# Six pairs of merge gates by seven block products, and 33 convolution taps by ScalarE and adding transfers, in a decoder layer on one core

## The chip, the core and the metric

The kernel runs on one core of a Trainium2 chip. Its engines are TensorE (PE in the profile, with its weight loads as PEld), VectorE (DVE), ScalarE (ACT), GpSimd (POOL) and SyncE (SP), which mostly issues transfers. The metric is the device time of one execution in microseconds (us). Three runs of the kernel before gave 833.68 to 834.18 us, with a median of 833.92.

## What is computed

One layer of a hybrid decoder trunk for 512 tokens (T) of width 1024 (D), all in float32. Cut to what matters here:

```python
u = rmsnorm(h, norm1_g)
a_glu, q, k, v, r, g_low, gate_a, gate_b = split(u @ w_in)

c = a_glu[..., :1024] * sigmoid(a_glu[..., 1024:])
c = causal_depthwise_conv(c, conv_dw_w, conv_dw_b)      # 31 taps along the tokens
c = silu(layernorm(c, conv_ln_g, conv_ln_b))
y_conv = c @ w_conv_out

o = gated_linear_attention(q, k, v, g_low)              # 4 heads, chunks of 64
y_gla = (head_rmsnorm(o) * silu(r)) @ w_gla_out

merged = sigmoid(gate_a) * y_conv + sigmoid(gate_b) * y_gla
h = h + merged @ w_o

u2 = rmsnorm(h, norm2_g)
z = causal_depthwise_conv(u2 @ w_ffn_up)                # 3 taps, 5632 columns
h = h + (silu(z[..., :2816]) * z[..., 2816:]) @ w_ffn_down
out = rmsnorm(h, final_g)
```

## The kernel before

**Precision.** Every product of float32 matrices is made of three matmuls (`mm3`, L405 to L407): each operand is split into a high part, the value rounded by a cast on ACT, and a low part, the difference taken by DVE; high x low, low x high and high x high are summed in PSUM.

**A plain tile** (`col_tile`, L409) makes 128 columns of a projection for all 512 tokens, channels in the partitions: eight blocks k of 128 input channels, three matmuls of 128x512 each, so 24 matmuls into one PSUM bank. `acts1` are the split activations u, `acts2` those of the FFN. The weight of a tile is one block of 128x1024 (512 KB), loaded by SP into a `raw` tile (four buffers); `split_weight` (L323) casts it into `whi` on ACT and subtracts into `wlo` on DVE (four buffers each).

**The order of the work** is written out in a list `order` of (weight, tile). `weight()` (L372) checks the list off, splits the weights up to two tiles ahead (LOOK) and then calls `fill(RATE)`. `refill` keeps four loads ahead, or two where `few` is true (in the seven-product part of the FFN, whose pairs need several raw tiles at once). The framework puts each engine's instructions in an order of its own within these bounds.

**The filling work.** `chains` is a list of lists of small operations for DVE that PE does not wait for at once. Each `fill(RATE)` puts some into the program, in turns from the first two chains: 31 taps of the depthwise convolution for each of 8 channel blocks (`conv_tap`, L703: the first by ACT into the tile `conv[k]`, the other 30 by DVE, at L711, one multiply-add each), and when all taps are done the chain of the convolution's norm (`norm_chain`, L796): sums over channels, mean on PE, centering and squares (L764, L770), variance on PE, 1/sigma by POOL (L455) and spread over the partitions by PE (L748), then for each block a multiply on DVE (L782), silu on ACT (L784), a cast on ACT and a subtract on DVE (L792, L793), which give `ca[k]`, the operand of w_conv.

**Stages on PE**, one after the other: the input's norm and u; half of v; 16 tiles of w_glu (the convolution's input); w_low and the decay gates (four activations at L841, exponentials at L845, logarithms at L847); the other half of v; four heads of gated attention with their w_qk and w_r tiles; then the merge; w_o; the FFN.

**The merge** (plain tiles only): four w_gb tiles in the last head; then eight w_gla tiles in turns with the last four w_gb; eight w_ga; eight w_conv. The sigmoids (L1021, L1030) are on ACT, the products with y on DVE. Each w_conv tile needs all eight blocks `ca[k]`, block by block in the order of its matmuls. `while chains: fill(1)` ahead of w_conv puts what is left of the chains into the program.

**Seven products.** A product of two 2x2 block matrices can be had from seven block products in place of eight. w_o and w_down are computed so (`seven`, L1075). In the FFN's up projection `up_pair` (L1308) does it for a pair of tiles: the weight blocks are combined by POOL (`up_sums`, L308, additions at L310) into x1, x3, x2 and x4 (x4 is half a block), the activations into s1, n2, s4 and n3 (`sum_acts`, L1248), and PE makes 7 x 4 x 3 = 84 matmuls of 128x256. Between the steps PE has halves of plain tiles, so that the copies (L1315) and combinations (L1318) of one step lie beside them. The combinations are put into the plan by `up_plan` (L147), with the kinds of unit "opens", "closes" and one without a name.

**Adding transfers.** A transfer issued by POOL can add to what stands at its destination (`accum_op`). The kernel before uses it to combine weight blocks of w_o and w_down (L300, L301), from DRAM into SBUF.

Of the kernel before, what the change touches and what calls it, by code (L numbers as in the profile page):

```python
# [17 lines left out]
P = 128  # L18
# [16 lines left out]
AHEAD = 4  # L35
LOOK = 2
# [30 lines left out]
def trunk_layer(ctx: ExitStack, tc: tile.TileContext, a: dict, out: bass.AP):  # L67
# [79 lines left out]
    def up_plan(gi):  # L147
# [8 lines left out]
        def unit(q, f, kind):  # L156
# [35 lines left out]
    def up_order(plan):  # L192
        out = []
        for what, i, *rest in plan:
            if what == "part":
                out.append(("w_up7", (i, rest[0])))
# [10 lines left out]
    order += [("w_gb", m) for m in range(AHEAD)]  # L207
    for m in range(KT):
        order += [("w_gla", m)] + [("w_gb", m + AHEAD)] * (m + AHEAD < KT)
    order += [("w_ga", m) for m in range(KT)]  # L210
    order += [("w_conv", m) for pair in O_PAIRS for m in pair]
    order += [("w_o", (O_PAIRS, step, d)) for step, d in STEPS]
    for gi, pairs in enumerate(GROUPS):
        if gi == 0:
            order += [("w_up", j) for i in pairs[0] for j in (i, FT + i)]
            first7 = len(order) + 6
        order += up_order(up_plan(gi))
        order += [("w_down", (pairs, step, d)) for step, d in STEPS]
# [6 lines left out]
    def load():  # L225
        if len(raws) < len(order):
# [4 lines left out]
            if name == "w_up7":  # L231
                q, part = j
                if part == "x1":
                    pair_raws[q] = [raw_tile() for _ in range(2)]
                    for raw, m in zip(pair_raws[q], (q, FT + q)):
                        nc.sync.dma_start(raw, a["w_up"][m])
# [6 lines left out]
    def refill():  # L243

        while len(raws) < len(order):
            few = len(raws) >= first7 and order[len(raws)][0] != "w_down"
            if len(raws) >= len(ready) + (2 if few else 4):
# [55 lines left out]
    def up_operand(q, part):  # L303

        raws = pair_raws[q]
        return {"x1": lambda: raws[0], "x3": lambda: raws[2], "x2": lambda: raws[1], "x4": lambda: raws[2][:, :T]}[part]()

    def up_sums(q, part):  # L308
# [3 lines left out]
        if part == "x1":  # L312
            one, two = pair_raws[q]
            three = raw_tile()
            pair_raws[q].append(three)
# [3 lines left out]
        if part == "x3":  # L319
            one, _, three = pair_raws[q]  # L320
            add(three[:, left], three[:, right], one[:, right])

    def split_weight(halves=False, between=None):  # L323

        if len(ready) < len(order):
# [4 lines left out]
            if name in SEVEN or name == "w_up7":  # L330
                raw = operand(raw, *spec) if name in SEVEN else up_operand(*spec)
# [5 lines left out]
                sum_on(name, *spec) if name in SEVEN else up_sums(*spec)  # L337
# [34 lines left out]
    def weight(name, j, ahead=LOOK):  # L372
# [4 lines left out]
        fill(RATE)  # L377
# [6 lines left out]

    def fill(n):
        room[0] += n
        while chains and room[0] > 0:
            room[1] += 1
            chain = chains[room[1] % min(2, len(chains))]
# [4 lines left out]
            if not chain:  # L394
                chains.remove(chain)
                if not chains and after:
# [304 lines left out]
    conv = [None] * KT  # L701

# [10 lines left out]
    for k in range(KT):  # L713
# [5 lines left out]
        nc.vector.tensor_tensor(c, pa, sg, ALU.mult)  # L719
        chains.append(  # L720
            [(1 if tap < CW - 1 else 0, lambda k=k, tap=tap, c=c: conv_tap(k, tap, c)) for tap in reversed(range(CW))]
        )

# [269 lines left out]

    heads = [Head(h) for h in range(HEADS)]
    for h in range(HEADS + 1):
# [7 lines left out]
        if old:  # L1003
            old.scores(heads[h - 2].gated if h > 1 else None)
        new.keys() if new else gate_b(1)
# [10 lines left out]

    part = [None] * KT
    ma = [None] * KT
    for m in range(KT):
        part[m] = heap()  # L1020
        nc.scalar.activation(part[m], gbs.pop(m), AF.Sigmoid)  # L1021
        py = col_tile(weight("w_gla", m), oa)
        if m + AHEAD < KT:
            gate_b(m + AHEAD)
        nc.vector.tensor_tensor(part[m], py, part[m], ALU.mult)
    gas = {}
    for m in range(KT):
        pg = col_tile(weight("w_ga", m), acts1)
        gas[m] = heap()
        nc.scalar.activation(gas[m], pg, AF.Sigmoid)  # L1030
    while chains:
        fill(1)
    H = T // 2

    def merged(m):
        sg = gas.pop(m)
        py = col_tile(weight("w_conv", m), ca)
        nc.vector.tensor_tensor(sg, py, sg, ALU.mult)
        nc.vector.tensor_tensor(sg, sg, part[m], ALU.add)
        return sg  # L1040
# [203 lines left out]


    seven_acts = {}

    def sum_acts():  # L1248


        def f32(x):
            return x.bitcast(F32)

        def part(t, k):
            return [u2[k][j][:, :, t * H : (t + 1) * H] for j in range(2)]

        a11, a12, a21, a22 = part(0, 0), part(0, 1), part(1, 0), part(1, 1)

        def tile(pool, tag, bufs, k=4):
            return pool.tile([P, k, H], F32R, tag=tag, name=nm(tag + "s"), bufs=bufs)  # L1260

        def chain(engine, out, start, *terms):

            for op, x in terms:
                engine.tensor_tensor(out, start if start.dtype == F32 else f32(start), f32(x), op)
                start = out
            return out

        def split_sum(src, his, lo):
            n = 4 // len(his)  # L1270
            for j, hi in enumerate(his):
                ks = slice(j * n, (j + 1) * n)
                nc.scalar.copy(hi, src[:, ks])
                nc.vector.tensor_tensor(lo[:, ks], src[:, ks], f32(hi), ALU.subtract)
            return [hi[:, k, :] for hi in his for k in range(n)], [lo[:, k, :] for k in range(4)]

        add, sub = ALU.add, ALU.subtract
        lo = {"n3": tile(fp, "us", 3), "s1": tile(fp, "us", 3), "n2": tile(fp, "us", 3), "s4": tile(tp, "x", 3)}
        hi = {"n3": [tile(tp, "btmp", 2, 2) for _ in range(2)], "s1": [tile(tp, "x", 3)]}
        hi |= {"n2": [tile(tp, "x", 3)], "s4": [tile(tp, "gain", 1)]}  # L1280

        def room(_):
            return keep_tile("w_down").rearrange("p (k t) -> p k t", k=4)

        src = {step: room(step) for step in ("s1", "n2")}
        chain(nc.vector, src["s1"], a21[0], (sub, a22[0]), (add, a21[1]), (sub, a22[1]))
        chain(nc.vector, src["n2"], src["s1"], (sub, a11[0]), (sub, a11[1]))
        yield
        for step in ("n2", "s1"):
            seven_acts[step] = split_sum(src[step], hi[step], lo[step])  # L1290
        yield
        src |= {step: room(step) for step in ("s4", "n3")}
        chain(nc.vector, src["s4"], src["n2"], (add, a12[0]), (add, a12[1]))
        chain(nc.vector, src["n3"], a11[0], (sub, a21[0]), (add, a11[1]), (sub, a21[1]))
        yield
        for step in ("n3", "s4"):
            seven_acts[step] = split_sum(src[step], hi[step], lo[step])
        for step, x in (("a11", a11), ("a12", a12), ("a22", a22)):
            seven_acts[step] = [[y[:, k, :] for k in range(4)] for y in x]
        yield  # L1300

    def up_step(acc, step, w, half, opens):
        ah, al = seven_acts[step]
        for k in range(4):
            s = slice(half * T + k * P, half * T + (k + 1) * P)
# [239 lines left out]
```

## Time and profile before

| | |
|---|---|
| median of three runs | 833.92 us (833.68 to 834.18) |
| the profiled execution | 833.95 us |
| its span | 832.2 us |
| granted clock of PE | 0.998 |
| w_gla's first matmul | 286.7 us |
| w_conv's first matmul | 398.0 us |
| last block of the convolution's norm ready | 399.6 us |
| w_o's first matmul | 441.5 us |

The profile is of one execution. Its page shows the busy time of each engine, the chain of work that ended last (followed back from the last instruction: at each step to what released it), the costliest groups of instructions by line, and the transfers. The trace behind it answers further questions: the waits of an engine by what ended them, the rows of a stretch of time (start, duration, engine, line, operation, output and inputs), and busy time by stage. L405 is line 405 of the kernel. A row's duration can overlap with the next row's, above all on PE; the spacing of starts is then what one costs.

### The profile page before, as it was taken

The page shows a single profiled execution, that of the slowest core. Times are in us where ns is not written, and L with a number is a line of the kernel's source. Part 1 is how long each engine was busy: PE and PEld are TensorE (multiplying, and loading weights), DVE is VectorE, ACT ScalarE, POOL GpSimd, SP SyncE. Part 2 cuts the span into 40 slices and gives each one's busy share as a digit, 9 for nine tenths or more (in the row PEclk, how much of TensorE's full clock was granted, in tenths as well). Part 3 has the DMA queues.
Part 4 walks back from the last instruction along what each step waited for, and adds up shares of the span by engine and source line. Part 5 has one row for each costly group of instructions (what it writes and reads, how often), then busy time and mean ns, then how long its engine had stood idle before and what let it go on. Part 6 is the DMA issues. An engine that isn't in the chain of part 4 may idle for free.

```text
span 832.2 us, 10782 instructions
## 1 busy us (share of the span) xinstructions
PE 822.1 (99%) x4109; PEld 699.8 (84%) x4109; DVE 697.7 (84%) x982; ACT 417.7 (50%) x597; POOL 98.1 (12%) x97
## 2 busy tenths in 40 slices
PE   9999999999999999999999999999999999999996
PEld 7888888888888888888888898898889888889885
DVE  5689879999998799745678889989985999789896
ACT  6723337547533422349544546556435564466654
POOL 2000000000001100000001100230133301513011
PEclk9999999999999999999999999999999999999999
DMA  8223232332212323323337623046632456224662
GB/s 313 101 99 103 84 104 80 98 102 76 93 65 96 117 86 101 102 76 101 102 85 221 190 86 102 26 158 168 143 123 93 142 137 162 104 93 165 174 126 101
DMA packets 28307, 97.82 MB, mean 118 GB/s; under 512 B 3209, under 2 KB 3345, under 8 KB 28257
## 3 DMA queue, kind: packets, MB, share of 16 engines
q1 hardware_dynamic: 24800, 85.35, 30.2%
q0 software_dynamic: 3456, 11.80, 8.4%
q8 instruction: 32, 0.52, 0.3%
q14 instruction: 19, 0.15, 0.1%
HBM read 95.03 MB, written 2.10 MB: 117 GB/s over the span
## 4 chain that ended last, share of the span: by engine, by line
PE 86%; DVE 5%; DMA 4%; issue 2%; ACT 1%; POOL 0%; SPq 0%; POOLq 0%; ACTq 0%; DVEq 0%
PE mm L405 24%; PE mm L406 24%; PE mm L407 24%; PE mm L617 3%; PE ax L405 2%; PE ax L407 2%; PE ax L406 2%; DMA kept<-in_w_o_dram 2%; DVE tmp L1199 1%; DVE wlo L336 1%; DMA raw<-in_w_down_dram 1%; DMA hres<-in_x_dram 1%; PE ax L958 1%; DVE hres L1119 1%; PE ax L960 1%
## 5 line engine op out<-in xcount | busy, mean ns | idle before, releaser
L405 PE MATMUL mm<-uh,wlo 128*128 128x512 f32 (+1 forms) x696 | 261.6, 376 | 0.0
L406 PE MATMUL mm<-ul,whi 128*128 128x512 f32 (+1 forms) x696 | 259.3, 373 | 0.0
L407 PE MATMUL mm<-uh,whi 128*128 128x512 f32 (+1 forms) x696 | 259.0, 372 | 0.0
L362 ACT CAST whi<-raw 128x1024 fp32r<-128x1024 f32 x98 | 102.5, 1048 | 126.3 <-PE mm L407 82.2
L711 DVE SCALAR_TENSOR_TENSOR c<-h,pp,c 128x511 f32<-128x511 f32 (+14 forms) x240 | 162.5, 729 | 0.7
L363 DVE TENSOR_TENSOR wlo<-raw,whi 128x1024 fp32r<-128x1024 f32 x98 | 123.3, 1261 | 35.6 <-ACT whi L362 35.4
L407 PEld LDWEIGHTS mm<-uh,whi 128*128 128x128 f32 x696 | 131.0, 188 | 23.3
L405 PEld LDWEIGHTS mm<-uh,wlo 128*128 128x128 f32 x696 | 131.2, 189 | 22.3
L406 PEld LDWEIGHTS mm<-ul,whi 128*128 128x128 f32 x696 | 131.2, 188 | 22.0
L336 DVE TENSOR_TENSOR wlo<-raw,whi 128x1024 fp32r<-128x1024 f32 (+1 forms) x56 | 65.0, 1167 | 16.5 <-ACT whi L335 12.6
L335 ACT CAST whi<-raw 128x1024 fp32r<-128x1024 f32 (+1 forms) x56 | 53.8, 964 | 28.2 <-PE mm L407 21.3
L310 POOL TENSOR_TENSOR raw<-raw,raw 128x512 f32<-128x512 f32 x24 | 38.3, 1597 | 144.6 <-DVE wlo L336 65.4
L335 ACT CAST whi<-kept 128x1024 fp32r<-128x1024 f32 (+1 forms) x32 | 31.8, 996 | 33.6 <-DVE kept L294 14.4
L1199 DVE SCALAR_TENSOR_TENSOR tmp<-mm,pp,tmp 128x511 f32<-128x511 f32 (+1 forms) x56 | 41.3, 740 | 4.6 <-ACT tmp L1197 4.5
L336 DVE TENSOR_TENSOR wlo<-kept,whi 128x1024 fp32r<-128x1024 f32 (+1 forms) x32 | 36.9, 1153 | 5.9 <-ACT whi L335 5.7
L455 POOL TENSOR_TENSOR rstd<-var,mhalf 128x2 f32<-128x2 f32 (+1 forms) x12 | 12.0, 1006 | 220.5 <-DVE var L965 196.3
L1119 DVE TENSOR_TENSOR hres<-hres,mm 128x512 f32<-128x512 f32 (+1 forms) x49 | 32.3, 669 | 1.7 <-PE mm L407 0.8
L1197 ACT ACTIVATE tmp<-mm,pp 128x512 f32<-128x512 f32 x28 | 21.7, 775 | 20.5 <-PE mm L407 20.4
L1199 DVE SCALAR_TENSOR_TENSOR tmp<-tmp,pp,tmp 128x511 f32<-128x511 f32 (+1 forms) x32 | 27.1, 904 | 0.1
L407 PE MATMUL mm<-whi,sh 128*128 128x512 f32 x66 | 25.7, 389 | 0.0
L406 PE MATMUL mm<-wlo,sh 128*128 128x512 f32 x66 | 25.7, 389 | 0.0
L405 PE MATMUL mm<-whi,sl 128*128 128x512 f32 x66 | 25.5, 389 | 0.0
(305 smaller groups left out, 1496.2 us busy)
## 6 DMA issues: line engine op xcount, KB each, us to landing
raw<-in_w_up_dram SPq DMA_DIRECT2D x44, 512.0 KB, 3.5
raw<-in_w_glu_dram SPq DMA_DIRECT2D x16, 512.0 KB, 3.6
raw<-in_w_down_dram SPq DMA_DIRECT2D x15, 512.0 KB, 4.2
kept<-in_w_down_dram POOLq DMA_DIRECT2D x10, 512.0 KB, 6.1
raw<-in_w_v_dram SPq DMA_DIRECT2D x8, 512.0 KB, 4.2
raw<-in_w_qk_dram SPq DMA_DIRECT2D x8, 512.0 KB, 3.3
raw<-in_w_r_dram SPq DMA_DIRECT2D x8, 512.0 KB, 3.3
raw<-in_w_gb_dram SPq DMA_DIRECT2D x8, 512.0 KB, 3.3
```

The lines of the kernel that those rows point to most:

```text
L310: add = lambda out, x, y: nc.gpsimd.tensor_tensor(out, x, y, ALU.add)
L335: nc.scalar.copy(hi, raw)
L336: nc.vector.tensor_tensor(lo, raw, hi.bitcast(F32), ALU.subtract)
L362: nc.scalar.copy(hi, raw)
L363: pace[0] = nc.vector.tensor_tensor(lo, raw, hi.bitcast(F32), ALU.subtract)
L405: nc.tensor.matmul(acc, ll, rh, start=first, stop=False, **kw)
L406: nc.tensor.matmul(acc, lh, rl, start=False, stop=False, **kw)
L407: nc.tensor.matmul(acc, lh, rh, start=False, stop=last, **kw)
L617: nc.tensor.matmul(acc, act, ready[k // 2][wi][:, j], start=first, stop=last)
L711: nc.vector.scalar_tensor_tensor(y[:, s:], c[:, : T - s], w, y[:, s:], ALU.mult, ALU.add)
L1119: nc.vector.tensor_tensor(hres[t, n][:, c], hres[t, n][:, c], acc[:, c], op)
L1199: nc.vector.scalar_tensor_tensor(z[:, s:], acc[:, : T - s], w[j], z[:, s:], ALU.mult, ALU.add)
```

## The change

It has two parts, with their consequences for the order.

1. **Gates by seven products.** Twelve of the sixteen gate tiles (w_gb 4 to 7, w_ga 0 to 7) are made as six pairs by seven products of 128x256 blocks, each pair in turns with two plain tiles cut into halves: the first three pairs with w_gla 2 to 7, the other three with w_conv (0 and 2, 1 and 3, 4 and 6). So w_conv begins in the fourth pair, and the last two w_conv tiles follow the pairs. The sums of activations s1, n2, s4 and n3 of u are made in pieces put into the program by `fill` ahead of the chains (`urgent`), in the last head and after. `up_pair`, `up_step`, `up_sums`, `up_operand` and `sum_acts` become `two_tiles`, `step_of_two`, `two_sums`, `two_operand` and `token_sums_7`, which the FFN uses as well.

2. **33 taps off DVE.** At each `fill`, while more than two convolution chains are there, up to two of the chains behind the first two give one tap to `tap_by_dma`: ACT multiplies the input by the tap's weight into one of two `products` buffers, and POOL issues a transfer that adds it to `conv[k]` (256 KB, from SBUF to SBUF). A chain that was served so rests for DVE until the next turn.

Besides: the number of chain operations for each tile changes (1.5 for a step of a pair, 6 for w_glu, 4 in the stretches with pairs, 5 elsewhere); loads are two ahead in all stretches with pairs; the FFN's unit "closes" cuts its first tile at 5 and 7 in place of 3 and 6; and the FFN's sums are placed after each "first" and "second".

```diff
+MERGE = [("w_gb", 4 + 2 * j, 5 + 2 * j, ("w_gla", 2 + 2 * j), ("w_gla", 3 + 2 * j)) for j in range(2)]
+MERGE += [("w_ga", 0, 1, ("w_gla", 6), ("w_gla", 7))]
+MERGE += [("w_ga", 2 * j + 2, 2 * j + 3, *(("w_conv", m) for m in O_PAIRS[j])) for j in range(3)]
+MERGE_REST = [("w_conv", m) for m in O_PAIRS[3]]
...
-                a1, a2, a3 = (("tile", a, ks) for ks in halves(3, 6))
+                a1, a2, a3 = (("tile", a, ks) for ks in halves(5, 7))
...
-    for m in range(KT):
-        order += [("w_gla", m)] + [("w_gb", m + AHEAD)] * (m + AHEAD < KT)
-    order += [("w_ga", m) for m in range(KT)]
-    order += [("w_conv", m) for pair in O_PAIRS for m in pair]
+    order += [("w_gb", m) for m in range(AHEAD)] + [("w_gla", m) for m in range(2)]
+    tight = set()
+    first = len(order)
+    for name, p, q, a_, b_ in MERGE:
+        x1, x3, x2, x4 = (("two", (name, p, q, part)) for part in ("x1", "x3", "x2", "x4"))
+        order += [x1, a_, x3, x2, b_, x4]
+    tight |= set(range(first, len(order)))
+    order += MERGE_REST
...
-        fill(RATE)
+        fill({"two": 1.5, "w_glu": RATE + 1}.get(name, RATE - (used[0] - 1 in tight)))
...
     def fill(n):
         room[0] += n
+        while urgent and room[0] > 0:
+            share, work = urgent.pop(0)
+            room[0] -= share
+            with tc.issue_after(pace[0].ins):
+                work()
+        if chain_of:
+            taps_by_dma(chains[2:])
         while chains and room[0] > 0:
             room[1] += 1
-            chain = chains[room[1] % min(2, len(chains))]
+            two = [chain for chain in chains[:2] if id(chain) not in resting] or chains[:1]
+            chain = two[room[1] % len(two)]
...
+    products = tp.tile([P, 2, T], F32, tag="gain", name=nm("products"), bufs=1)
+    turn, last = [0], [[]]
+
+    def taps_by_dma(waiting):
+
+        waiting = sorted((c for c in waiting if id(c) not in last[0]), key=len)[-2:]
+        resting[:] = [*last[0], *map(id, waiting)]
+        last[0] = [id(c) for c in waiting]
+        for chain in waiting:
+            tap_by_dma(chain)
+
+    def tap_by_dma(chain):
+
+        k = chain_of[id(chain)]
+        while chain[0][0] == 0:
+            chain.pop(0)[1]()
+        tap = len(chain) - 1
+        chain.pop(0)
+        n = T - (CW - 1 - tap)
+        turn[0] += 1
+        y = products[:, turn[0] % 2, :n]
+        w = pp[:, PP_CW + k * CW + tap : PP_CW + k * CW + tap + 1]
+        with tc.issue_after(pace[0].ins):
+            nc.scalar.activation(y, conv_in[k][:, :n], AF.Copy, scale=w)
+        nc.gpsimd.dma_start(conv[k][:, T - n :], y, accum_op=ALU.add)
...
+        s1 = chain("s1", a21[0], (sub, a22[0]), (add, a21[1]), (sub, a22[1]))
+        n2 = chain("n2", "s1", (sub, a11[0]), (sub, a11[1]))
+        s4 = chain("s4", "n2", (add, a12[0]), (add, a12[1]))
+        n3 = chain("n3", a11[0], (sub, a21[0]), (add, a11[1]), (sub, a21[1]))
+        return acts7, [s1 + n2, split_sum("s1"), s4, split_sum("n2"), split_sum("s4"), n3, split_sum("n3")]
...
+    def pair_7(name, p, q, a_, b_):
+        unit = two_tiles(name, p, q, lambda: merge_acts, mm_bank)
+        low, high = range(KT // 2), range(KT // 2, KT)
+        if a_[0] == "w_conv":
+            while chains:
+                fill(1)
+        next(unit)
+        acc = tile_of(*a_, low)
+        next(unit)
+        tile_of(*a_, high, acc)
+        next(unit)
+        acc = tile_of(*b_, low)
+        for m, c in zip((p, q), next(unit)):
+            (part if name == "w_gb" else gas)[m] = sigmoid(m, c)
+        tile_of(*b_, high, acc)
+
+    for spec in MERGE[:3]:
+        pair_7(*spec)
```

Each `next(unit)` makes one step of the pair: x1 with two of the seven products, x3 with two, x2 with two, x4 with one.

More of the change, by code (lines that the diff above doesn't have):

```diff
@@ L1014, in trunk_layer @@
     late_scope, late = scoped("late", 1, "right")
+    for work in merge_sums[2:]:
+        urgent += work
     part = [None] * KT
[L1018 to L1024, printed above, removed]
-        nc.vector.tensor_tensor(part[m], py, part[m], ALU.mult)
[L1026 to L1030, printed above, removed]
@@ L1243, in second_of_pair @@
         return acts
[L1246 to L1300, printed above, removed]
```

232 lines of the change are left out of this document (166 added, 66 removed).

## The prediction

> **What bounds the kernel now.** I read the busy totals first, then the chain that ended last, then the waits of TensorE (PE), then single stages in the timeline.
>
> ```profile
> PE 822.1 (99%) x4109; PEld 699.8 (84%) x4109; DVE 697.7 (84%) x982; ACT 417.7 (50%) x597; POOL 98.1 (12%) x97
> ...
> PE 86%; DVE 5%; DMA 4%; issue 2%; ACT 1%; POOL 0%; SPq 0%; POOLq 0%; ACTq 0%; DVEq 0%
> ```
>
> PE is busy in 99% of the span and makes 86% of the chain. What it waited for, in the view of PE's waits (total, times, longest):
>
> ```profile
> PE mm L523 <- DVE ones L496: 1.1, 1, 1.1
> PE ax L531 <- DMA x<-in_x_dram: 0.8, 1, 0.8
> PE mm L405 <- ACT tmp L1315: 0.7, 2, 0.4
> PE ax L484 <- DVE ul L489: 0.3, 1, 0.3
> ```
>
> That is 2.9 us in 832.2, nearly all before 10 us and after 475 us. In the merge PE waits for nothing, so matmul time taken out there counts one for one, unless another engine becomes late. The profiled execution took 833.95 us, its span 832.2 (1.75 us lie outside); the median of the runs is 833.92, so the sum below may stand against either.
>
> **Part 1, the seven products.** Their price is in the trace, since the FFN of the kernel before already works in this way. PE starts, us:
>
> ```profile
> 538.64 0.39 PE L406 MATMUL mm<-ul,whi 128*128 128x512 f32 x1
> 538.87 0.39 PE L407 MATMUL mm<-uh,whi 128*128 128x512 f32 x1
> 539.10 0.28 PE L405 MATMUL mm<-uh,wlo 128*128 128x256 f32 x1
> 539.21 0.28 PE L406 MATMUL mm<-ul,whi 128*128 128x256 f32 x1
> ...
> 541.97 0.40 PE L405 MATMUL mm<-uh,wlo 128*128 128x512 f32 x1
> ```
>
> The second column overlaps (pipelined), so I take spacings. 512 columns: 538.87 - 538.64 = 0.23 (0.2267 over a long run). 256 columns: 24 in 541.97 - 539.10 = 2.87, or 0.1197 each. A plain tile is 24 x 0.2267 = 5.44. A pair by seven is 7 x 12 = 84 narrow matmuls, 84 x 0.1197 = 10.05, in place of 2 x 5.44 = 10.88. The saving is 0.83 by product; from one x1 to the next x1 the FFN shows 560.14 - 539.10 = 21.04 for a pair with two plain tiles in halves, against 4 x 5.44 = 21.76: 0.72. I take 0.72, which holds the switches. Six pairs: **-4.3 us**. The matmul count of everything else is the same.
>
> What the pairs add on other engines. VectorE (DVE) forms the sums of the activations (14 operations of 128x1024 at a spacing of 1.14 = 16 us), 1.7 us more of weight splitting per pair (3.5 in place of 2 at 1.14), and 1.0 of combining (3 at 0.34). ScalarE (ACT) gets 1.5 us of casts and 1.3 of copies per pair, and 4 us for the sums. POOL gets four additions per pair (1.3 to 2.3 each, L310), on an engine that is 12% busy. Each pair with its two plain tiles lasts 21 us on PE. In the first pair DVE's own work (splits 6.3, sums, combines, chain) comes to about 25 us in those 21, but in the trace the wlo splits there run 17 to 20 us ahead of PE's use (250 to 290 us), so 5 to 8 us of lead remain: **0**.
>
> DVE loses some of its speed beside POOL:
>
> ```profile
> 543.73 1.30 POOL L310 TENSOR_TENSOR raw<-raw,raw 128x512 f32<-128x512 f32 x1 [10.03 <-DVE wlo L336]
> ...
> 544.15 1.43 DVE L1210 TENSOR_TENSOR w<-tmp,tmp 128x512 f32<-128x512 f32 x1
> ```
>
> The same L1210 takes 0.75 us elsewhere, so one collision costs about 0.7, and four in each pair would cost 24 x 0.7 = 17. The view of busy time by stage shows what is free there (columns: stage, its length, then busy time of PE, PEld, DVE, ACT, POOL):
>
> ```profile
> 286.00:398.00 112.00, 112.00 (x508) 93.06 (x507) 77.95 (x106) 55.59 (x70) 1.01 (x1) 1.00 0.28 90
> 398.00:441.00 43.00, 43.00 (x191) 35.63 (x190) 31.67 (x49) 17.66 (x24) 1.94 (x2) 1.00 0.41 107
> ```
>
> DVE has 34 + 11 = 45 us free there, and gets 32 more (16 + 10 + 6) less the taps of part 2. I keep 0; if that cover fails, the norm is late (part 3).
>
> **Part 2, 33 convolution taps off DVE.** They are what makes room for those sums:
>
> ```profile
> L711 DVE SCALAR_TENSOR_TENSOR c<-h,pp,c 128x511 f32<-128x511 f32 (+14 forms) x240 | 162.5, 729 | 0.7
> ```
>
> Spacing in a run of them is 0.65 us, so 33 give back 21.5 us. Summed over the program DVE goes from 663.9 to 675.7 us of such durations: still 84% or so of the span, in other places. In return ACT multiplies 33 times (0.6 to 0.7 each by its 128x512 activations) and POOL issues 33 adding transfers of 256 KB. No transfer from SBUF to SBUF is in the trace. The nearest are POOL's adding transfers of weights:
>
> ```profile
> raw<-in_w_down_dram POOLq DMA_DIRECT2D x1, 256.0 KB, 3.6
> kept<-in_w_down_dram POOLq DMA_DIRECT2D x1, 256.0 KB, 7.8
> ```
>
> 3.6 us from issue to landing alone, 7.8 behind others. I take 3.6, since mostly one or two fly; both ends stay. There are two buffers of products, so a multiply waits until the transfer two before it has landed, and a transfer waits for the one before it on its chain. Queued behind a waiting multiply on ACT are the casts whi, and PE waits for those. The tightest place is the gates: three taps stand between the four L841 activations, and two landings in a row are ahead of the last. In the trace the four start at 131.94; by 3.6 the last starts near 137.8, then two table loads (1.28 each), eight activations (2.20 per four) and the cast whi, now near 147.6 for a tile PE reaches at 153.4. With the cast, the subtract and DVE's queue ahead of it, some 2 us are left: **0** at 3.6, a wait from about 4.6 on. Later taps (six of the last chain, 155 to 180 us) have over 7 us.
>
> The Trainium skill, page "SBUF — State Buffer", section "SBUF: two separate sides", speaks against such transfers: descriptors of a POOL-queued DMA are made by GpSimd and starve while a DVE operation in a two-port mode holds the port they share. In this trace such issues take 0.84 to 0.9 us with DVE at work, a few 1.06 to 1.25, so starvation is not seen; by the page the slower rival's sum below would come out, by the row the sum is unchanged.
>
> **Part 3, the order of the merge.** In the trace the convolution's norm is finished only just in time. First ACT, then DVE, from the spread of 1/sigma (L748) on:
>
> ```profile
> 371.72 1.28 ACT L784 ACT_TABLE_LOAD   x1
> 373.01 1.52 ACT L784 ACTIVATE btmp<-c,pp 128x512 f32<-128x512 f32 x2
> 374.44 1.12 ACT L792 CAST ch<-btmp 128x512 fp32r<-128x512 f32 x2
> ```
>
> ```profile
> 370.95 1.29 DVE L782 TENSOR_TENSOR c<-ax,c 128x512 f32<-128x512 f32 x2 [4.49 <-PE ax L748]
> ...
> 398.87 0.69 DVE L793 TENSOR_TENSOR c<-btmp,ch 128x512 fp32r<-128x512 f32 x1
> ```
>
> The first w_conv tile starts at 398.0 and the last normed block is ready at 399.56, 29 us after the spread at 370.0. After the change the w_conv tiles stand among the pairs: the first comes at 286.7 (first w_gla) + 43.5 (eight w_gla tiles at 5.44) + 30.2 (three pairs at 10.05) + 2.9 (the next x1) = 363.3, some 35 us earlier, and the norm must come earlier too. The spread (call its end T) now stands in the third pair, before a half tile (2.75), x4 (1.43), a half (2.75) and the next x1 (2.87): the first convolution block is wanted at T + 9.8. The eighth is wanted after 27 more wide and 24 narrow matmuls: 27 x 0.2267 + 24 x 0.1197 = 9.0, so T + 18.8 to 19.2. ACT needs from T on: a cast whi (0.96), a table load (1.28), two silu (1.43), two casts (1.05), a copy (0.3); then the next whi, whose buffer comes free when PE is done with x4 and a half tile, T + 7.4; then 0.96, a load 1.28, two sigmoids 1.0, a load 1.28, two silu and the casts: the third block at T + 13.9, wanted at T + 12.2; the rest (two silu, two casts, whi, copy, twice more) ends at T + 21.6. **PE waits 1.7 us at the third block and 3.0 in all by the eighth.** The ends: 0, if the scheduled spread runs ahead of this (PE reaches it late, ACT having been idle), and 3.1. I take 2.4, midway between 1.7, which follows from the first load of tables, and 3.0, which needs every later step in its place.
>
> SP's queue holds 175 instructions as before. The kept w_o loads move behind the w_conv loads in it, since the sums hold their buffers until the last pair; the w_o loads land in 3.3 to 5.8 us there, and are due later than that by my count: 0. In the FFN the halves of one kind of unit are cut at 5 and 7 and not 3 and 6: same matmuls, 0.
>
> **Sum**: 833.95 - 4.3 + 2.4 = **832.0 us**.
>
> **Rivals.**
> - All is hidden: no wait at w_conv, 833.95 - 4.3 = **829.6**. For it: waits in the merge are nil now and ACT is half idle. Against it: the chain above is a row of dependent steps.
> - DVE is late in the merge as well: the sums, the collisions with POOL and the norm (two 0.6 us passes over eight blocks) share DVE, so T slips against PE. One collision each in the norm's sums, centering and last multiplies makes 3 x 0.7 = 2.1 more: **834**, no change.
> - Slower: ACT is held by the landings. It decides above 4.6 us from issue. At 7.0 (two in flight) the last gate activation is 2 x 3.4 = 6.8 later, less the 2 us left: 4.8, and PE stands still that long at 153 us; with the sum, 832.0 + 4.8 = **836.8**. For it: 7.8 in the row above. Against it: that transfer was queued behind two larger ones.
>
> **How the numbers follow.** 0.2% (1.7 us) is about what a measurement can tell from no change: faster is below 832.25, slower above 835.6. The forecast has 0.42, of which about two thirds lie below 832.25; all hidden 0.18; DVE late 0.15; landings 0.25. Faster 0.46, same 0.29, slower 0.25. The range runs from 829.4 to 836.8, which leaves out half of the landings' case and a little on the other side.
>
> **What would show it.** Right: x1 to x1 of 21.0 us with two plain tiles in the merge; a wait of PE for ch or c in the first w_conv tile of 1.7 to 3; no wait of PE at 150 to 195 us. Wrong: PE waiting for whi or wlo near 153 us, transfers c<-products landing in over 4.6 us; L363 late in the first pair; or more than 3 us before the first w_conv tile.

## The result, and the profile after

The changed kernel takes 849.22 us (median of four runs, 847.97 to 849.66) against 834.05 for the kernel before: the ratio is 1.0177, with an interval of 1.0159 to 1.0195. The forecast was 832.0, with a range up to 836.8; it is slower by 15 us where a small gain was expected.

The profiled execution of the changed kernel took 849.16 us, its span 847.4, so 15.2 us more than the span before. Busy times, the chain by engine, and two groups of the page (line, engine, operation, tiles and count; busy, mean ns of one; idle time before it and what ended most of it):

```profile
PE 823.8 (97%) x4325; PEld 705.9 (83%) x4325; DVE 720.1 (85%) x1001; ACT 452.1 (53%) x669; POOL 165.9 (20%) x154
...
PE 69%; DVE 12%; DMA 6%; issue 6%; ACT 5%; POOL 1%; POOLq 0%; SPq 0%; ACTq 0%; DVEq 0%
...
L747 POOL DMA_DIRECT2D c<-products x33 | 28.9, 899 | 143.2 <-ACT products L746 112.1
...
L746 ACT ACTIVATE products<-h,pp 128x511 f32<-128x511 f32 (+9 forms) x33 | 23.3, 717 | 43.1 <-DMA c<-products 43.1
```

PE's share of the chain fell from 86% to 69%. The last line names the new thing: ScalarE (ACT) stood still for 43.1 us ahead of 18 of its 33 multiplies, each time until a transfer `c<-products` had landed. PE's waits in the changed kernel, the four largest (total, times, longest):

```profile
PE mm L425 <- DVE wlo L373: 5.7, 4, 2.2
PE ax L886 <- DVE h L877: 2.8, 1, 2.8
PE ax L988 <- ACT kt L968: 2.1, 1, 2.1
PE ax L1023 <- ACT o L1017: 1.6, 1, 1.6
```

None of these is in the list of before. In the stage of the gates and the first head they end at 132.5, 152.2, 160.0, 173.6 and 195.0 us. To place all losses I add up, from the trace's PE rows, what the spacing of successive matmuls exceeds its usual value (0.227 us for 512 columns, 0.120 for 256). This is what PE lost, by stage, in us (differences of under 1 us mean little); the medians are beside it:

| kernel | median | 128-200 us (gates, v, first head) | 200-310 (other heads) | 360-410 (norm and first w_conv tiles) |
|---|---|---|---|---|
| before | 834.05 | 0.5 | 1.5 | 0.2 |
| changed | 849.22 | 15.1 | 5.1 | 1.7 |
| e1, taps on DVE | 854.91 | 0.5 | 3.9 | 18.4 |
| e4, no transfers | 836.44 | 0.5 | 6.1 | 1.6 |
| e10, three pairs, nine taps | 833.77 | 0.5 | 2.3 | 0.2 |
| e14, no transfers, first pair later | 831.63 | 0.5 | 1.6 | 0.8 |
| e15, transfers apart | 850.03 | 14.9 | 6.3 | 1.7 |
| e16, the same, memset on DVE | 838.43 | 0.5 | 8.8 | 1.7 |

Over the whole span the changed kernel lost 20.0 us more of this than before (25.2 against 5.2), and its span grew by 15.2, so the seven products gave back 4.8, near the 4.3 of the forecast. Their rate is in the trace, PE rows of the changed kernel from one x1 to the next (start, duration):

```profile
314.94 0.28 PE L425 MATMUL mm<-uh,wlo 128*128 128x256 f32 x1
...
335.98 0.62 PE L809 MATMUL ax<-sum,shares 128*128 128x512 f32 x2
336.44 0.28 PE L425 MATMUL mm<-uh,wlo 128*128 128x256 f32 x1
```

Without the two matmuls of the norm's mean that stand between, 335.98 - 314.94 = 21.04 us for this pair and two plain tiles, the figure taken from the FFN.

### The profile page after: what moved, and what is told of

Same layout as the page of the kernel before. It is cut to its first block, busy times and chain, and to the rows that moved or that the text cites. A ratio compares the mean times of both kernels' runs of the same rounds, so it can differ in the third digit from the quotient of the medians.

```text
span 847.4 us, 11474 instructions
## 1 busy us (share of the span) xinstructions
PE 823.8 (97%) x4325; PEld 705.9 (83%) x4325; DVE 720.1 (85%) x1001; ACT 452.1 (53%) x669; POOL 165.9 (20%) x154
## 4 chain that ended last, share of the span: by engine, by line
PE 69%; DVE 12%; DMA 6%; issue 6%; ACT 5%; POOL 1%; POOLq 0%; SPq 0%; ACTq 0%; DVEq 0%
PE mm L425 19%; PE mm L426 19%; PE mm L427 19%; DMA c<-products 6%; DVE c L757 5%; PE mm L637 3%; PE ax L427 2%; PE ax L425 2%; PE ax L426 2%; DVE wlo L373 2%; DVE tmp L1416 1%; DVE wlo L346 1%; POOL c L747 1%; ACT whi L372 1%; ACT products L746 1%
## 5 line engine op out<-in xcount | busy, mean ns | idle before, releaser
L426 PE MATMUL mm<-ul,whi 128*128 128x512 f32 (+1 forms) x672 | 243.3, 362 | 0.0
L427 PE MATMUL mm<-uh,whi 128*128 128x512 f32 (+1 forms) x672 | 242.9, 361 | 0.0
L757 DVE SCALAR_TENSOR_TENSOR c<-h,pp,c 128x499 f32<-128x499 f32 (+22 forms) x207 | 141.8, 734 | 0.7
L373 DVE TENSOR_TENSOR wlo<-raw,whi 128x1024 fp32r<-128x1024 f32 x86 | 108.6, 1265 | 17.6 <-ACT whi L372 17.5
L372 ACT CAST whi<-raw 128x1024 fp32r<-128x1024 f32 x86 | 89.6, 1046 | 57.0 <-PE mm L427 33.9
L346 DVE TENSOR_TENSOR wlo<-raw,whi 128x1024 fp32r<-128x1024 f32 x80 | 95.3, 1195 | 29.0 <-ACT whi L345 25.0
L320 POOL TENSOR_TENSOR raw<-raw,raw 128x512 f32<-128x512 f32 x42 | 64.4, 1533 | 244.6 <-DVE wlo L346 151.2
L345 ACT CAST whi<-raw 128x1024 fp32r<-128x1024 f32 x80 | 76.5, 958 | 38.5 <-PE mm L427 23.2
L747 POOL DMA_DIRECT2D c<-products x33 | 28.9, 899 | 143.2 <-ACT products L746 112.1
L746 ACT ACTIVATE products<-h,pp 128x511 f32<-128x511 f32 (+9 forms) x33 | 23.3, 717 | 43.1 <-DMA c<-products 43.1
L1117 ACT COPY tmp<-mm 128x256 f32<-128x256 f32 x48 | 17.6, 369 | 43.9 <-PE mm L427 43.6
L320 POOL TENSOR_TENSOR raw<-raw 128x512 f32<-128x512 f32 x14 | 29.1, 2080 | 0.0
```

The source lines that it names most:

```text
L320: add = lambda out, x, y: nc.gpsimd.tensor_tensor(out, x, y, ALU.add)
L345: nc.scalar.copy(hi, raw)
L346: nc.vector.tensor_tensor(lo, raw, hi.bitcast(F32), ALU.subtract)
L372: nc.scalar.copy(hi, raw)
L373: pace[0] = nc.vector.tensor_tensor(lo, raw, hi.bitcast(F32), ALU.subtract)
L426: nc.tensor.matmul(acc, lh, rl, start=False, stop=False, **kw)
```

## The experiments

Each run stood beside the kernel before on the same chip, which took 833.1 to 833.8 us there; the ratios are to that.

**Where is the loss: transfers, multiplies or sums?**

e1, the changed kernel with all taps back on DVE:

```diff
-        if chain_of:
-            taps_by_dma(chains[2:])
```

> The changed kernel with all taps back on DVE; seven products and everything else as changed. Theory 1 (ScalarE is held by the landings of the 33 adding transfers: 43.1 us of waits ahead of its multiplies, which PE feels as 14.7 us more idle time at 128 to 200 us): that loss goes, 849.2 - 14.7 = 834.5, plus what 33 x 0.65 = 21.5 us more of DVE work make late at w_conv, at most some 7: 834 to 842, and no wait of PE at 150 to 200 us. Theory 3 (the sums and splits of the seven products overload DVE, the transfers do no harm): 849 or more, with the waits at 290 to 400 us.

854.91 us, ratio 1.0253 (1.0233 to 1.0273): neither. PE lost only 0.5 us at 128 to 200, so the loss there does belong to the transfers; but the taps on DVE cost more than the 7 us allowed for, at another place:

```profile
PE mm L423 <- DVE wlo L346: 4.9, 1, 4.9
PE mm L423 <- ACT ch L838: 4.2, 1, 4.2
```

These are waits at the norm and the first w_conv tiles, 18.4 us in that stage. So the change trades one loss for another of about the same size: the w_conv tiles are wanted some 29 us earlier (the first at 369.3 us in e4, below, against 398.0 before), and DVE does not have the norm ready unless the 33 taps go elsewhere.

e2, the kernel before with the taps by transfers alone (the functions `taps_by_dma` and `tap_by_dma`, and the call in `fill`; 39 taps go this way and not 33, presumably since w_glu keeps its old number of chain operations):

> The kernel before with the 33 taps by ScalarE and adding transfers, and none of the seven products in the merge. Theory 1: 834 + 13 to 15 = 847 to 849, with ScalarE waiting some 40 us for landings. Theory 3: 834 or a little less, since DVE has 21.5 us less to do.

861.72 us, ratio 1.0335 (1.0317 to 1.0352), ScalarE waiting 54.7 us for landings: the transfers do harm without any seven products, and more than expected.

e3, six buffers of products:

```diff
-    products = tp.tile([P, 2, T], F32, tag="gain", name=nm("products"), bufs=1)
+    products = [tp.tile([P, 2, T], F32, tag=tag, name=nm("products"), bufs=n) for tag, n in (("gain", 1), ("x", 3), ("x", 3))]
...
-        y = products[:, turn[0] % 2, :n]
+        y = products[turn[0] // 2 % 3][:, turn[0] % 2, :n]
```

> The changed kernel with six buffers of products in place of two, so that a multiply need not wait for the transfer two before it; the transfers still wait for the one before them on their chain. Theory 1, with the buffers as the place: ScalarE's 43 us of waits fall to under 15, and the time to 835 to 840. Theory 1, with the order on a chain as the place (POOL holds the next transfer): little change, 845 to 849. Theory 2 (the 33 multiplies themselves, 24 us of ScalarE time, push the casts back): 849.

859.47 us, ratio 1.0309 (1.0287 to 1.0331): slower than with two, which no theory had. ScalarE's waits fell to 33.4 us but in 11 pieces, the longest 9.7. The transfers still went mostly one behind another, the first at 70.9 us and the last at 185.0: 3.6 us apart in the mean, against 3.9 with two buffers. More buffers hardly made the queue of transfers faster. Why this kernel is slower still is not shown: the four buffers more are taken from tiles that other stages use too (tag x), and PE lost some 3 us already ahead of 128 us.

e4, the multiplies kept, the transfers left out:

```diff
-        nc.gpsimd.dma_start(conv[k][:, T - n :], y, accum_op=ALU.add)
```

> The changed kernel with the 33 multiplies kept on ScalarE and their transfers left out, so that 33 taps are missing from the convolution. Theory 1: 849.2 - 14.7 = 834.5 or so. Theory 2 (the multiplies' own time and their places in ScalarE's order): 845 to 849.

836.44 us, ratio 1.0024 (1.0011 to 1.0038). The multiplies' own 23 us on ScalarE cost nothing at 128 to 200 us; about 12.8 us are bound to the transfers.

**Which transfers?** e5 and e6 issue only some of the 33, with all multiplies in place:

```diff
+        if used[0] <= order.index(("w_low", 0)):     # e5; e6 has > in place of <=
+            nc.gpsimd.dma_start(conv[k][:, T - n :], y, accum_op=ALU.add)
```

> The changed kernel with all 33 multiplies, but only the 11 transfers issued up to the last w_glu tile; the 22 later ones are left out, so 22 taps are missing. If ScalarE's lateness builds up in the GLU stage already (theory 1a, since its first waits stand at 75 to 128 us), PE's first 3.0 us of idle time at 129 us remains and some of what follows: 839 to 842. If only the waits among the gate activations count (theory 1b, the prediction's arithmetic), 836.4, as without any transfers.

> The changed kernel with all 33 multiplies, but only the 22 transfers issued from w_low on; the 11 earlier ones are left out, so 11 taps are missing. Theory 1a: ScalarE comes to the gates on time and loses about 7 us among them, of which the slack hides most: 838 to 842, with no PE wait at 129 us, and the losses of this run and of the other half do not add up to 12.8. Theory 1b: nearly the whole 12.8 us stay, 847 to 849.

e5: 840.50 us, ratio 1.0074 (1.0048 to 1.0100); e6: 850.93, ratio 1.0207 (1.0174 to 1.0240). The early ones cost 4 us as theory 1a has it, with a wait of PE of 3.0 us that ends at 134 (its four runs spread from 837.9 to 842.9); the late ones alone cost all, which by the time is 1b. The two losses, 4.1 and 14.5, add up to more than the 12.8. In e6 ScalarE is on time at 118 us and waits 12.8 us for landings by 139.7, so the stretch right ahead of and in the gates is enough for the loss; lateness from the w_glu stage is not needed.

**Other costs.** e7 is e4 with the sums put into the program after the last head:

```diff
-            if not new:
-                urgent += [*merge_sums[0], *merge_sums[1]]
-                hold.append(True)
...
-    for work in merge_sums[2:]:
+    hold.append(True)
+    for work in merge_sums:
         urgent += work
```

> As the run without transfers (33 taps missing), but the sums s1 and n2 of the activations are put into the program after the last head and not in it. Theory: the 4 us that PE waits in the last head for o (behind var, which stands behind the sums on DVE) go, but the first pair then may wait for s1 or n2: 833 to 836. Rival (the wait there is from DVE being slowed by POOL's additions): unchanged at 836.4.

836.77 us, ratio 1.0032 (1.0020 to 1.0045): unchanged, as the rival says. PE still waited 3.0 us for o in the last head. More on this at e14, below.

e8, a complete kernel with three pairs, the sums placed as in e7, all taps on DVE, and w_conv last as before:

```diff
+FIRST = [("w_gla", 0), ("w_gb", 4), ("w_gla", 1), ("w_gb", 5), ("w_gb", 6), ("w_gb", 7)]
+MERGE = [("w_ga", 2 * j, 2 * j + 1, ("w_gla", 2 * j + 2), ("w_gla", 2 * j + 3)) for j in range(3)]
+MERGE_REST = [("w_ga", 6), ("w_ga", 7)] + [("w_conv", m) for pair in O_PAIRS for m in pair]
```

> A complete kernel: all taps on DVE, only w_ga 0 to 5 as three pairs in turns with w_gla 2 to 7, after the plain w_gb tiles, and the w_conv tiles last as in the kernel before; sums after the last head. If the seven products are worth 0.8 us a pair wherever DVE has room and the norm is not wanted earlier: 834.0 - 2.4 + up to 1 = 831.5 to 832.5. If the 16 us of sums make the norm late at w_conv anyway: 836 to 842.

840.34 us, ratio 1.0066 (1.0051 to 1.0082). PE lost 6.8 us at the first w_conv tile: even with w_conv last, the pairs' work on DVE makes the norm late.

**Does the rate decide?** e9 gives at most one tap a fill to the transfers (`[-2:]` becomes `[-1:]`):

> The changed kernel with at most one tap given to ScalarE and a transfer at each fill, not two: 26 transfers, 7 taps back on DVE; complete. Theory 1c (the rate: 33 transfers one after the other in 124 us are 3.75 us each, which is their landing time, so two per 5.4 us of PE do not fit and one does): ScalarE's waits fall from 43 us to under 12, PE's idle time at 128 to 200 us from 15 to under 5, and the total to 838 to 842. Theory 1d (each wait costs what it costs, whatever the rate): waits of 26/33 x 43 = 34 us, 12 us of PE idle time there, and 846 to 850.

845.98 us, ratio 1.0158 (1.0134 to 1.0183), waits of 24.6 us, 11.4 us lost at 128 to 200 (in the profile, which is of the slowest of the four runs, 849.27 us). That is 1d much more than 1c. The multiplies are not evenly spread: three waits of 4 to 5 us each stand again at 118 to 142 us.

e10, three pairs (e8) with nine taps by transfers, one a fill, only while w_glu is computed; e11, the changed kernel with its transfers only while w_glu is computed:

```diff
-        if chain_of:
+        if chain_of and used[0] < 21:
             taps_by_dma(chains[2:])
```

> A complete kernel: three pairs as in the run with three pairs, and nine taps by ScalarE and transfers, one at a fill and only while w_glu is computed. PE waited 6.8 us at the first w_conv tile there, for the norm. If that is DVE's work, 9 x 0.65 = 5.9 us less of it bring the total from 840.3 to 834.5 to 836.5, with no PE wait at 128 to 200 us; if it is the norm's own steps, it stays at 839 to 841.

> The changed kernel (six pairs), with the 11 taps by transfers that are issued while w_glu is computed, two at a fill, and none after; complete, 22 taps back on DVE. PE's idle time at 128 to 200 us as with the early transfers alone (5.2 us); and at w_conv some 18.4 x 22/33 = 12 us of the 18.4 that all taps on DVE cost: 849 to 853. If the taps on DVE cost nothing until a threshold: 840 to 845.

e10: 833.77 us, ratio 1.0009 (0.9998 to 1.0020). ScalarE waited 0.9 us in all, PE's 6.8 us at w_conv went to 0.2. It is no faster than the kernel before. e11: 847.15 us, ratio 1.0165 (1.0150 to 1.0180), with 1.3 us lost at 128 to 200, where 5.2 had been expected, and 13.1 at the norm. With e1 (33 taps, 18.4), e9 (7 taps, 2.0) and the changed kernel (none, 1.7), a tap on DVE in the six-pair kernel costs about 0.5 us of PE's time beyond the first seven.

**Is it the wait or the transfer?** e12 moves the multiplies to POOL; e13 does so for three pairs and one tap a fill:

```diff
-            nc.scalar.activation(y, conv_in[k][:, :n], AF.Copy, scale=w)
+            nc.gpsimd.tensor_scalar(y, conv_in[k][:, :n], w, None, ALU.mult)
```

> The changed kernel with the 33 multiplies on POOL in place of ScalarE; transfers, buffers and order on the chains as changed; complete. Theory 1 (the loss comes from waits that stand in ScalarE's queue ahead of casts and gate activations): PE's idle time at 128 to 200 us falls from 15.1 to under 3, and the total to 836 to 839. Rival (landings, or the later taps on the same chain, hold PE by way of DVE, which needs the sums in conv; or POOL's work slows DVE as its additions do): 843 to 850, with DVE's taps above 0.9 us at 70 to 200 us.

> A complete kernel: the three pairs of w_ga with w_gla, and one tap at a fill (26) by POOL's multiplies and transfers. If POOL's multiplies leave ScalarE free and DVE undisturbed, DVE has 17 us less to do than with three pairs alone: 831.5 to 833. If DVE is slowed by them as beside POOL's additions (0.7 us each): 834 to 842.

e12: 872.32 us, ratio 1.0470 (1.0451 to 1.0489); e13: 846.93, ratio 1.0155 (1.0112 to 1.0199). Both expectations fell. DVE's taps kept their 0.73 us in the median; the 69 of 207 in e12 that ran beside a multiply of POOL took 0.85 in the mean against 0.74, some 7 us in all. The large losses lie elsewhere. PE waited 16.2 us in one piece in e12 (6.0 in e13), for a small DVE subtract (L877 in e12). It stood in DVE's order behind one that needed the gates' weights, and their loads wait for a memset of POOL (L862). In e12's POOL queue that memset ran at 137.0 us, where the kernel before has it at 79.7. A second wait of 8.2 us in e12, until 218 us, is for a DVE copy (L992) behind a tap ahead of which DVE stood still for 7.7 us; what that tap waited for, the profile does not name.

e15 keeps multiplies and transfers but takes the dependence between them away (so the weights of these 33 taps are left out):

```diff
-        nc.gpsimd.dma_start(conv[k][:, T - n :], y, accum_op=ALU.add)
+        nc.gpsimd.dma_start(conv[k][:, T - n :], conv_in[k][:, :n], accum_op=ALU.add)
```

> The changed kernel with the 33 multiplies on ScalarE and the 33 transfers, but the transfers add the unmultiplied input, so that no multiply waits for a transfer and none for a multiply (the weights of these 33 taps are left out). Bytes, order on the chains and POOL's queue stay. Theory 1 (the wait in ScalarE's queue is the loss): PE idle at 128 to 200 us under 2 us and 835.5 to 838. Rival (the transfers themselves, by what they do to DVE's taps, to other transfers or to POOL's other work): 845 to 850.

850.03 us, ratio 1.0198 (1.0177 to 1.0220): by its time this is the rival. But PE lost nearly all of it at one point. The rows of POOL, of SP's and of ScalarE's queue, and PE's wait:

```profile
131.00 0.84 POOL L862 MEMSET tmp<- 128x512 f32 x1
131.87 2.19 SPq L864 DMA_DIRECT2D tmp<-in_gate_up_dram  x5
...
137.48 0.62 ACT L865 CAST gate_up<-tmp 128x512 fp32r<-128x512 f32 x1 [14.68 <-DMA tmp<-in_gate_up_dram]
```

```profile
PE ax L886 <- DVE h L877: 13.0, 1, 13.0
```

The memset had stood in POOL's queue behind transfers that each waited for the one before on its chain (78.2 us of such waits, 27 times); after it come five loads, ScalarE's cast (idle 14.68 us), a DVE subtract, PE. So e16 is the same with that memset on DVE, and e17 is the changed kernel itself with it on DVE:

```diff
-    nc.gpsimd.memset(raw, 0.0)
+    nc.vector.memset(raw, 0.0)
```

> As the run with multiplies and transfers apart (the 33 taps unweighted), with the memset for the gates' weights on DVE in place of POOL. There PE lost 13.1 us at one point, 129 us, behind that memset in POOL's queue, and 0.4 us at 143 to 200 us. Theory 1e (a wait for a landing costs what stands behind it in the queue of the engine that waits; on ScalarE casts and gate activations, on POOL this memset): PE idle at 128 to 200 us under 1.5 us, 835.5 to 838. Rival (the transfers by themselves cost the 13 us, at another place then): 845 to 850.

> The changed kernel, complete, with only that memset on DVE. In the changed kernel the memset runs at 115 us and the cast that waits for it at 126 us, behind multiplies; so theory 1e expects little: 846 to 849, with ScalarE's waits for landings still about 40 us. If the memset is what costs in the changed kernel as well: 836 to 840.

e16: 838.43 us, ratio 1.0065 (1.0045 to 1.0086), and 0.5 us lost at 128 to 200. 33 transfers and 33 multiplies run beside everything at no cost there, once nothing that PE needs stands behind a wait for a landing; the 2 us over e4 lie in the heads. e17: 852.42 us, ratio 1.0230 (1.0207 to 1.0253), ScalarE's waits 44.8 us: in the changed kernel the memset is not the place; the multiplies in ScalarE's queue are. Theory 1e has both, though e17 is 3 us slower than it allowed and than the changed kernel, which stays open.

**The last head, and a faster version?** e14 is e4 with w_gb 4 and 5 as plain tiles, so that the first pair of five comes later, after two more plain tiles; the sums stay in the last head. e18 has four pairs of w_ga, w_conv last, nine taps, and the memset on DVE.

```diff
+FIRST = [("w_gla", 0), ("w_gb", 4), ("w_gla", 1), ("w_gb", 5)]
+MERGE = [("w_gb", 6, 7, ("w_gla", 2), ("w_gla", 3))]                                    # e14
+MERGE += [("w_ga", 2 * j, 2 * j + 1, ("w_gla", 2 * j + 4), ("w_gla", 2 * j + 5)) for j in range(2)]
+MERGE += [("w_ga", 2 * j + 4, 2 * j + 5, *(("w_conv", m) for m in O_PAIRS[j])) for j in range(2)]
...
+MERGE = [("w_ga", 2 * j, 2 * j + 1, ("w_gb", j + 6), ("w_gla", j + 2)) for j in range(2)]   # e18
+MERGE += [("w_ga", 2 * j, 2 * j + 1, ("w_gla", 2 * j), ("w_gla", 2 * j + 1)) for j in (2, 3)]
```

> As the run without transfers (33 taps missing), with w_gb 4 and 5 as plain tiles and the first pair two tiles after the last head; the sums stay in the last head. Theory 2 (PE's 4 us in the last head come from DVE being slowed by POOL's additions for the first pair): that wait falls under 1 us, and the total from 836.4 by 3 to 4 less 0.8 for the pair given up: 833 to 834. Rival (the sums in DVE's queue ahead of var): the wait stays at 2 to 4 us, and the total at 836.5 to 837.5.

> A complete kernel: all of w_ga as four pairs, in turns with w_gb 6 and 7 and w_gla 2 to 7, first pair four tiles after the last head, w_conv last; nine taps by transfers, one at a fill while w_glu is computed; the memset on DVE. With three pairs this stood at 833.8, even with the kernel before. A fourth pair gives 0.8 us on PE and 2.7 us more to DVE ahead of the norm: 833 to 835.

e14: 831.63 us, ratio 0.9974 (0.9964 to 0.9984), with no wait for o left in the last head. e7 without the sums there still has the wait, and e14 without the additions there has none, so POOL's additions and not the sums made it. With 33 taps missing it is a bound and no version to use. e18: 842.76 us, ratio 1.0105 (1.0088 to 1.0122), where 833 to 835 was expected, with 6.9 us lost at the first w_conv tiles: with a fourth pair DVE was late again (the longest wait, 3.2 us, is for a `wlo`). No complete kernel of the study is faster than the one before.

## Why the prediction was wrong

**The seven products, -4.3: right.** The spacing from x1 to x1 is 21.04 us, and PE's losses against the span leave 4.8 for the six pairs.

**33 taps, "0 at 3.6": the step that failed.** The landings themselves were forecast well: 3.7 us in the median, 3.2 to 5.8. The stretch that the prediction looked at also came out: from the first gate activation (L889 in the changed kernel) to the last it took 6.1 us, and 5.9 by the prediction (131.94 to 137.8; it does not show from where its two landings count). ScalarE's rows:

```profile
140.13 0.72 ACT L746 ACTIVATE products<-h,pp 128x510 f32<-128x510 f32 x1 [4.09 <-DMA c<-products]
140.76 0.67 ACT L889 ACTIVATE h<-ax,pp 128x512 f32<-128x512 f32 x1
143.98 0.72 ACT L746 ACTIVATE products<-h,pp 128x509 f32<-128x509 f32 x1 [2.55 <-DMA c<-products]
144.61 0.67 ACT L889 ACTIVATE h<-ax,pp 128x512 f32<-128x512 f32 x1
145.63 0.72 ACT L746 ACTIVATE products<-h,pp 128x508 f32<-128x508 f32 x1 [0.35 <-DMA c<-products]
146.26 0.67 ACT L889 ACTIVATE h<-ax,pp 128x512 f32<-128x512 f32 x1
146.83 0.68 ACT L889 ACTIVATE h<-mm,pp 128x512 f32<-128x512 f32 x1
```

What was not counted stands ahead of the first of them, which started at 140.76 us and not at 131.94. Six waits for landings precede it: 4.94 at 119 us, then 2.29, 1.09, 1.77, 0.52 and the 4.09 of the first row, together 14.7, of which a part fell into time that ScalarE had free before. So the last gate activation started at 146.83 and not at 137.8, and the 2 us that were left were gone. The same was missed behind the gates, where the prediction gave the later taps "over 7 us": ScalarE waited another 14.2 us at 159 to 190. With 2.9 us between the gate activations and 11.3 at 99 to 111 the 18 waits make 43.1 us, where the prediction had two landings, 7.2 us.

The mistake was to treat each transfer as a delay with slack before and after it. The 33 issues run from 70.0 to 193.7 us, 3.9 us apart in the mean, which is also the mean of their landing times. POOL's queue keeps its order, a transfer waits there for its multiply and for the one before it on its chain, and the multiplies wait for buffers. Two transfers were in flight for only 26 of the 127 us, so the whole row works much like one slow engine that ScalarE had to keep step with. e6 shows that the late part of it suffices, e9 that at most one a fill (26 of the 33) doesn't cure it, e3 that buffers don't, e16 that the same transfers cost nothing at 128 to 200 us when nothing that PE needs is behind such a wait.

**The slower rival: the right mechanism, mis-sized.** It put 4.8 us on landings of 7.0 and nothing below 4.6. It cost about 14.6 us (15.1 less 0.5) at 3.7. Part of that is PE's clock after a wait, which no term of the sum had; see the last section.

**DVE's collisions with POOL, "I keep 0": wrong in the last head.** The lead of wlo did cover wlo: PE waits for none there. But the first pair's additions fall into the last head, where DVE's `var` has no lead. DVE, POOL and ScalarE of the changed kernel:

```profile
289.79 1.58 DVE L757 SCALAR_TENSOR_TENSOR c<-h,pp,c 128x489 f32<-128x489 f32 x1
...
291.68 1.35 DVE L757 SCALAR_TENSOR_TENSOR c<-h,pp,c 128x488 f32<-128x488 f32 x1
292.96 1.75 DVE L1075 TENSOR_TENSOR btmpq<-xq,uh 128x512 f32<-128x512 f32 x1
...
298.89 0.15 DVE L1013 TENSOR_SCALAR var<-ss 128x2 f32<-128x2 f32 x1
```

```profile
289.56 2.96 POOL L320 TENSOR_TENSOR raw<-raw,raw 128x512 f32<-128x512 f32 x2 [18.14 <-DVE wlo L373]
292.47 1.69 POOL L320 TENSOR_TENSOR raw<-raw 128x512 f32<-128x512 f32 x1
```

```profile
300.23 0.84 ACT L1017 ACTIVATE o<-ax,rstd 128x256 f32<-128x256 f32 x2 [4.51 <-POOL rstd L475]
```

The taps take 0.73 us elsewhere and 1.58 and 1.35 here, the sum 0.68 and 1.75, some 2.5 us more in all; `var` is late, rstd and o behind it, and PE lost 3.2 us at 286 to 310. The Trainium skill, page "SBUF — State Buffer", section "SBUF: two separate sides", says that a DVE operation with two SBUF inputs and a GpSimd operation that reads SBUF exclude each other at a shared port. These rows agree, and e14, which moves the additions, removed the wait. In e12, beside POOL's multiplies (one tensor input), DVE's taps stayed at 0.73 us in the median, 1.80 at most, and POOL's own operations took from 1.55 to 5.40. The prediction let DVE's work grow by 11.8 us (its terms add up to 10.7); its busy time grew by 22.4, from 697.7 to 720.1, of which no run says how much is collisions.

**Starvation of POOL's transfers.** The other rule of that section of the Trainium skill (page "SBUF — State Buffer", section "SBUF: two separate sides"), that descriptors of POOL-queued transfers starve while a DVE operation in a two-port mode holds the shared port, was weighed in the prediction. This case does not show it: issues took 0.87 us in the median, and landings 3.7, with DVE busy for 123 of the 140 us from 60 to 200. It does not test it either, since no row tells whether any of DVE's operations there ran in a two-port mode.

**The norm's wait, +2.4: mis-sized, and not at the block forecast.** PE lost 1.5 us there (1.7 less 0.2), none of it at the third block. Of the 1.7 some 0.4 went at the fifth (at 389 us), 0.8 for the weights of the second w_conv tile (until 391.36; their cast whi, at 389.00, stood on ScalarE between silus and casts of the norm), and 0.5 for a combination ahead of the next pair (until 398.82). In e7, with the sums later, it was gone. "All is hidden" put 0 there and is off by the same 1.5. e1 shows that with the 33 taps on DVE this stage would have cost 18 us: they are what makes room for the sums, as the prediction has it.

Together: -4.3 + 14.6 + 3.6 (heads) + 1.5 + 0.3 elsewhere = 15.7, against 15.2 measured.

## What to carry to other kernels

A slow step that is taken off a busy engine is paid for in the queue of the engine that waits for it: count every instruction behind the wait, from the first such wait on, and not only the tightest place. Transfers that must follow one another are an engine of their own; compare their number times their landing time with the stretch they are in. And before work is moved between engines, look for what small thing (a memset, a `var`) stands behind it in the order of the receiving engine.

## What the runs showed of the hardware

After some of its waits PE ran at half speed for a while. PE waited 2.10 us until 160.0 in the changed kernel. Rows after that, and PE's view by stretches (busy time, granted clock, DMA share, GB/s):

```profile
160.78 0.40 PE L425 MATMUL mm<-uh,wlo 128*128 128x512 f32 x1
...
161.95 0.63 PE L426 MATMUL mm<-ul,whi 128*128 128x512 f32 x1
162.38 0.63 PE L427 MATMUL mm<-uh,whi 128*128 128x512 f32 x1
```

```profile
157.00:161.00 4.00, 1.90 (x8) 1.00 0.82 139
161.00:165.00 4.00, 4.00 (x12) 0.57 0.85 216
```

Matmuls that stand 0.23 us apart stood 0.43 apart for about 3 us, at a granted clock of 0.57: some 1.5 us more for a wait of 2.1. The same came after the wait of 2.15 us at 195 us, so about 3 of the 15.1 us at 128 to 200 are this. But two other waits of this size in the same stage, 2.83 us until 132.45 and 2.20 until 152.16, were not followed by it: the granted clock was 1.00 at 132 to 136 and at 154 to 157. In the 20 traces together each of the 21 waits of PE over 2.9 us (between 20 and 800 us) came with a stretch of half clock, and 15 of the 20 waits of 1.9 to 2.9 us did. What decides for the shorter ones is not shown.

The Trainium skill, page "TensorE: Matmul & The Clock Gate", section "Part 1: The HAM clock gate (the 'warmup' mystery)", has the clock at half after an idle window of some 3.4 us; here a wait of 2.10 us was enough, and the one of 2.20 us, 8 us ahead of it, was not.
